# Where six of the first sixteen weight sums run: out of the recurrence and the first MLP, into the output projection

## The chip, the cores and the metric

One core of one Trainium2 chip runs the whole program. The metric is the device time of one execution in microseconds; lower is better. The kernel before took 2056.83 us, the median of three runs (2054.85, 2056.83 and 2059.17 us).

## The reference

A trunk of two layers on one sequence of 1024 tokens with 1024 features, all in float32. Layer 0 mixes tokens by a gated linear recurrence (HGRN2), layer 1 by a Conformer convolution module. Each mixer is followed by a squared-ReLU MLP with 4096 hidden features.

```python
def reference(x, ...):
    for i in range(DEPTH):                       # DEPTH = 2
        if i % N_MIXERS == 0:
            mix = hgrn2_mixer(x, a_w_in[j], lb_all[j], a_norm_g[j], a_w_out[j])
        else:
            mix = conformer_conv_mixer(x, ...)
        x = layer_norm(DEEPNORM_ALPHA * x + mix, ln_mix_g[i], ln_mix_b[i])
        ff = jnp.square(jax.nn.relu(x @ ffn_w1[i])) @ ffn_w2[i]
        x = layer_norm(DEEPNORM_ALPHA * x + ff, ln_ffn_g[i], ln_ffn_b[i])
    return x

def hgrn2_mixer(h, w_in, lb, norm_g, w_out):
    ...                                          # chunks of 32, o per head
    o = o * lax.rsqrt(jnp.mean(jnp.square(o), axis=-1, keepdims=True) + RMS_EPS)
    ...
    return o.astype(h.dtype) @ w_out             # "output projection"
```

## The kernel before

Every large product is made in three passes: each operand is split into a high part that TensorE takes in one pass and a low part that holds the rest, and high x high, high x low and low x high are added in PSUM. On top of that the products of the two MLPs and of the recurrence's projections are made by a scheme of the Strassen kind: a product of 2 x 2 blocks becomes seven products ("forms", numbered 1 to 7) of sums of blocks. Forms 1, 2 and 4 take a block of the weight as it is; forms 6, 5, 7 and 3 take sums of two to four blocks.

**Weight sums.** The weights w2 of both MLPs' second products are cut into blocks; there are eight groups (c = 0 to 7) in each layer, four blocks of 128 x 1024 in each group. The four sums of a group are made in DRAM, by DMAs alone. `block_sums` (L402) issues them: two copies of 1 MiB from the weights into the sum's tile (L419, L420), then one addition of 1 MiB onto it (L421) and two additions of 0.5 MiB (L423), which each take what the one before left. [...] Sixteen such sums are made over the program: `to_sum` (L427) lists the eight of layer 0, then the eight of layer 1. Layer 0's are read in the first MLP's second product, from about 850 us on, and layer 1's in the last one, from about 1720 us on.

**Where they are issued.** Twelve in the recurrence: its loop over pairs p and forms i calls `block_sums` at every sixth form (L1022), with a gap of 12 ticks between the parts (a tick is one step of the recurrence's order; `later` puts a job that many ticks ahead). There POOL issues copies and additions alike. Two in the first MLP's loop over c, at c = 0 and c = 2 (L1477), with the copies on SP's queue and the additions on POOL's at once. The last two come later, in the second layer, through the argument `adds`; that is not touched.

**The output projection** (L1206 to L1220) runs over two halves of the tokens, four tiles t of 128 tokens in each and two column halves n: sixteen entries, of which entry 0, 1 and 2 had their product made in the recurrence's last steps (`early_out`). An entry makes a product of 24 matmuls (`w<-oT` in the trace), then DVE evacuates it into y. At n = 1 the layer norm of that tile follows (`x1_block`): statistics on DVE, a power on POOL (`mv<-mv,nhalf`, L518 in the trace, 1.5 us each), two DVE operations `y<-y,mv,ln_mix_g` and `y<-y,mv,ln_mix_b`, a store of y to DRAM for the residual (`kept<-y`, SP's queue), and TensorE transposes of y (`ps<-ident,y`) that become the operand `x1f` of the first MLP. Eight norms, so eight powers.

**Loads ahead.** In the same stretch SP loads the first weights of the first MLP (`raw<-in_w1q_dram`, L90 in `Slots`, L135 in `Forms`), which ACT and DVE split into `fw`; `early[0].ahead(1)` asks for the first of them at entry 9, the others follow at the end of the loop. Then form (0,1), (0,2), (1,1), (1,2) of the first MLP run (the pair is the group c and the form), and its loop goes on with form (0,6), the first one whose weight is a sum (`fw<-sum`), made by DVE from the loads.

**What sets the order.** In the recurrence the order of all engines' queues is the order of the code (`order` opens a manual schedule, closed at L1038). Behind L1038 a scheduler orders each engine's instructions by its own estimates. POOL, as any engine, runs its queue in order: an addition that waits for its copies holds up every power behind it.

Of the kernel before, what the change touches and what calls it, by code (L numbers as in the profile page):

```python
# [8 lines left out]
F32 = mybir.dt.float32  # L9
# [3 lines left out]
ALU = mybir.AluOpType  # L13
PSUM = bass.MemoryType.PSUM

P = 128
# [4 lines left out]
HT = 512  # L21
# [23 lines left out]
ORDER = (1, 2, 6, 5, 7, 3, 4)  # L45
# [66 lines left out]
class Forms(Slots):  # L112
# [12 lines left out]
    def add(self, x, y, out=None):  # L125
        out = self.sums() if out is None else out
        self.vector.tensor_tensor(out=out, in0=x, in1=y, op=ALU.add)
        return out
# [140 lines left out]
def body(ctx, tc, d, out):  # L269
    nc = tc.nc  # L270
    cst = ctx.enter_context(tc.tile_pool(name="cst", bufs=1))
    stat = ctx.enter_context(tc.tile_pool(name="stat", bufs=4))
    dram = ctx.enter_context(tc.tile_pool(name="dram", bufs=1, space=bass.MemoryType.DRAM))
# [6 lines left out]
    def view(kb, shape, dt=F32, name="t"):  # L280
        at, top = int(kb * 1024), KBYTES * 1024
        if at < edge[0]:
            if edge[0] < top:
                space.tile([P, (top - edge[0]) // 4], F32, name="gap")
            edge[0] = 0
        if at > edge[0]:
            space.tile([P, (at - edge[0]) // 4], F32, name="gap")
        edge[0] = at + (prod(shape) + 7) // 8 * 32
        return space.tile([P, *shape], dt, name=name)
# [39 lines left out]
    def acc():  # L329
        return rings["mm"]()  # L330
# [40 lines left out]
    order = ExitStack()  # L371
# [12 lines left out]
    def later(n, job):  # L384
        if n:
            waiting.append((ticks[0] + n, job))
        else:
            job()

    def tick(n=1):  # L390
        for _ in range(n):
            ticks[0] += 1
            for at, job in [w for w in waiting if w[0] <= ticks[0]]:
                waiting.remove((at, job))
                job()

    sums = {}

    def block_sums(name, layer, c, after=None, gap=0, adds=None):

        t = sums[name, layer, c] = dram.tile([4, P, 1024], F32, name=f"sum_{name}{layer}{c}")
        v, w = t.rearrange("a p n -> p a n"), d[name][layer, c].rearrange("a p n -> p a n")  # L402
        queue = nc.sync if after is not None else nc.gpsimd
        if adds is not None:

            def copies(rows, after):
                nc.sync.dma_start(out=t[0:4:2, rows.start, 0:1], in_=after)
                queue.dma_start(out=v[rows, 0:2], in_=w[rows, 0:4:2])
                queue.dma_start(out=v[rows, 2:4], in_=w[rows, 0:2])

            copies(slice(16, P), after)
            adds.append(lambda after: copies(slice(0, 16), after))
            adds.append(lambda after: nc.gpsimd.dma_start(out=v[:, 0:2], in_=w[:, 2:4], accum_op=ALU.add))
            for i in (2, 3):
                adds.append(lambda after, i=i: nc.gpsimd.dma_start(out=v[:, i], in_=v[:, i - 1], accum_op=ALU.add, max_dma_last_dim=4096))
            return
        if after is not None:
            nc.sync.dma_start(out=t[0:4:2, 0, 0:1], in_=after)
        queue.dma_start(out=v[:, 0:2], in_=w[:, 0:4:2])  # L419
        later(gap // 2, lambda: queue.dma_start(out=v[:, 2:4], in_=w[:, 0:2]))  # L420
        parts = [lambda: nc.gpsimd.dma_start(out=v[:, 0:2], in_=w[:, 2:4], accum_op=ALU.add)]  # L421
        for i in (2, 3):
            parts.append(lambda i=i: nc.gpsimd.dma_start(out=v[:, i], in_=v[:, i - 1], accum_op=ALU.add, max_dma_last_dim=4096))  # L423
        for i, part in enumerate(parts):
            later((i + 1) * gap, part)

    to_sum = [(*of, c) for of in (("w2", 0), ("w2", 1)) for c in range(NFC)]  # L427

# [72 lines left out]
    for k in range(4):  # L501
        c = slice((k % 2) * HT, (k % 2 + 1) * HT)
# [380 lines left out]
    def step():  # L883
        if recs and (not active or len(active) == 1 and active[0][2] >= LAG):
            active.append([recs[0], recurrence(recs.pop(0)), 0])
        if not active:
            return False
        if not (len(active) == 1 and active[0][0] == H - 1 and active[0][2] >= LAG):
            alone[0] = not alone[0]
            if alone[0]:  # L890
                return True
        for one in list(active):
            one[2] += 1

            def go(one=one):
                if next(one[1], one) is one:
                    active.remove(one)

            later(1 if one is not active[0] and one[2] <= 6 else 0, go)
        return True  # L900
# [68 lines left out]
    def seam():  # L969
        plan = [  # L970
            (5, lambda: fetch(0, 0)), (15, lambda: split_w(0, 0, 136)), (17, lambda: split_w(0, 1, 144)), (19, lambda: split_w(0, 3, 120)),
            (21, lambda: split_w(0, 2, 152)), (13, lambda: heads_in(0, 0, 4, 32)), (19, lambda: heads_in(0, 4, 6, 32)),
            (24, lambda: split_heads(0, 0)), (26, lambda: split_heads(0, 2)), (29, lambda: split_heads(0, 4)),
            (16, lambda: bring(0)), (17, lambda: bring(1)), (27, lambda: last_in(H - 2, 0, sixth[0])), (36, lambda: last_in(H - 1, 0, lastly[0])),
            (21, lambda: heads_in(1, 0, 6, 64)), (38, lambda: split_heads(1, 0)), (41, lambda: split_heads(1, 2)), (44, lambda: split_heads(1, 4)),
            (25, lambda: fetch(1, 80)), (39, lambda: split_w(1, 0, 112)), (42, lambda: split_w(1, 1, 128)),
            (45, lambda: split_w(1, 2, 96)), (47, lambda: split_w(1, 3, 104)),
            (43, lambda: last_in(H - 2, 1, sixth[1])), (46, lambda: last_in(H - 1, 1, lastly[1])),
        ]
        for n, job in plan:  # L980
            later(n, job)
# [25 lines left out]
    for p, (kind, j) in enumerate(PAIRS):  # L1007
        st = {"banks": dict(turn_of)}
        turn_of = {"z": turn_of["a"], "a": turn_of["b"], "b": turn_of["z"]}
        pace[1] = 0.0 if p == 0 else 0.6 if p < 3 else 0.5  # L1010
        if kind == "g" and p < len(PAIRS) - 1:
            to_load += [(2 * j, 0), (2 * j + 1, 1), (2 * j, 1), (2 * j + 1, 0)]
        if p == len(PAIRS) - 1:
            seam()
        for i in ORDER:
            if kind == "q" and i == 2:
                while any(a[0] <= j - 3 for a in active) or recs and recs[0] <= j - 3:
                    tick()
                    step()
            pair_product(p, i, made.pop(0), st)  # L1020
            later(2, make_form)
            if (7 * p + ORDER.index(i)) % 6 == 1 and len(to_sum) > 4:  # L1022
                block_sums(*to_sum.pop(0), gap=12)
        if kind == "q":
            later(4, lambda j=j: recs.append(j))
    early_out = ((0, 0), (1, 0), (2, 0))
# [9 lines left out]
    tick(100)  # L1036
    assert not waiting and not loaded and not to_load and not gates, (waiting, gates)
    order.close()  # L1038
    oT = [o[0] for o in oT]


# [94 lines left out]
    y = [view(160 + 16 * h, (NTB, D), F32, "y") for h in range(2)][::-1]  # L1136
# [57 lines left out]
    def x1_block(half, t):  # L1194
# [8 lines left out]
        if t < NTB - 1:  # L1203
            bg.chores += [lambda: x1_first(t), lambda: x1_second(t)]

    for half in range(2):  # L1206
        for t, n in early_out + ((0, 1), (1, 1), (3, 0), (2, 1), (3, 1)) if half == 0 else [(t, n) for t in range(NTB) for n in range(2)]:
            ps = acc()
            if half or (t, n) not in early_out:
                product(ps, wide(oT[half], t, ws[n]))  # L1210
            yv = y[half][:, t, n * HT : (n + 1) * HT]
            vector.scalar_tensor_tensor(out=yv, in0=yv, scalar=ALPHA, in1=ps, op0=ALU.mult, op1=ALU.add)
            if n == 1:
                if half == 1 and t == 0:
                    early[0].ahead(1)
                x1_block(half, t)
                if half == 0 and t:
                    bg.chore()
    for e in early[1:]:
        e.ahead(2)  # L1220


    def store(layer, c, i, q, src):
# [246 lines left out]
    for c in range(NFC):  # L1470
        for i in ORDER[2 if c < 2 else 0 :]:
            (f,) = fw.take(1)
            fw.ahead(3)
            if (c, i) == (0, 7):
                bg.done()
            up.form(c, i, f)
        if c in (0, 2):  # L1477
            block_sums(*to_sum.pop(0), f[:2, 1, :1].bitcast(F32))
        if c == 0:
            up.settle(1)  # L1480
            hold += [view(208, (2, 1024), F32, "spare"), view(216, (1024,), F32, "next")]


    y = [view(32 + 16 * h, (NTB, D), F32, "y") for h in range(2)]
# [371 lines left out]
    y = [view(kb, (NTB, D), F32, "y") for kb in (88, 112)]  # L1856
# [103 lines left out]
```

## Time and profile before

| | us |
|---|---|
| median of three runs | 2056.83 |
| the profiled execution | 2057.16 |
| its span, first to last instruction | 2055.4 |
| granted TensorE clock, mean | 0.999 |
| TensorE (PE) busy | 2023.6 |
| VectorE (DVE) busy | 1488.1 |
| ScalarE (ACT) busy | 1094.5 |
| GpSimd (POOL) busy | 396.3 |

How to read it: the span runs from the first to the last instruction of the profiled execution, and 1.76 us lie around it. A stretch "85 to 430" is counted in microseconds from the start of the span. The recurrence takes about 85 to 437, the output projection about 437 to 509, the first MLP's first product follows. "Idle before" is the time an engine stood still ahead of an instruction, with what ended it behind the arrow. Lines of DVE and PE read L204, a helper that records them, so they are told apart by the names of their tiles. The share of DMA is the mean busy share of the core's 16 DMA engines.

### The profile page before, as it was taken

How to read it: one execution, taken by the hardware profiler on the slowest of the kernel's cores; microseconds unless marked ns; L12 is line 12 of the kernel's file. 1: busy time of each engine (PE TensorE's matmuls, PEld its weight loads, DVE VectorE, ACT ScalarE, POOL GpSimd, SP SyncE). 2: the span in 40 equal slices, each digit the busy share in tenths (PEclk: the TensorE clock that was granted, in tenths of full speed). 3: DMA queues.
4: the chain of work that ended last, by engine and by line, in shares of the span. 5: the costliest groups of instructions: out<-in, count | busy, mean ns of one | idle time of the engine just before them, and what ended most of it. 6: DMA issues, size and time to landing. Idle time of an engine off the chain costs nothing. (4 is left out here: it accounts for less than half of the span.)

```text
span 2055.4 us, 29649 instructions
## 1 busy us (share of the span) xinstructions
PE 2023.6 (98%) x11144; PEld 1669.0 (81%) x11144; DVE 1488.1 (72%) x1978; ACT 1094.5 (53%) x1725; POOL 396.3 (19%) x405
## 2 busy tenths in 40 slices
PE   8999999999999999999999999999999999999998
PEld 7888887888787888888888888888888878888886
DVE  8698888877856675665567897889589666754456
ACT  5456565631655556444443776498615555443343
POOL 0112232111101000000001798089110000100002
PEclk9999999999999999999999999999999999999999
DMA  4778999842679776989998744496759768995542
GB/s 187 221 201 229 265 254 269 248 183 85 192 268 295 281 282 225 394 329 329 338 335 299 298 185 184 180 351 247 276 216 337 231 225 303 391 292 195 195 154 103
DMA packets 183944, 517.55 MB, mean 252 GB/s; under 512 B 17912, under 2 KB 49784, under 8 KB 182776
## 3 DMA queue, kind: packets, MB, share of 16 engines
q1 hardware_dynamic: 168312, 456.93, 61.7%
q0 software_dynamic: 15488, 58.72, 12.2%
q8 instruction: 87, 1.43, 0.3%
q14 instruction: 57, 0.47, 0.1%
HBM read 380.85 MB, written 201.85 MB: 283 GB/s over the span
## 5 line engine op out<-in xcount | busy, mean ns | idle before, releaser
L204 PE MATMUL ps<-dw,dh 128*128 128x512 f32 x2688 | 611.3, 389 | 0.5 <-DVE dh L204 0.5
L204 PEld LDWEIGHTS ps<-dw,dh 128*128 128x128 f32 x2688 | 504.3, 188 | 105.3 <-DVE dh L204 0.9
L204 PE MATMUL ps<-x1f,fw 128*128 128x512 f32 x1344 | 307.5, 390 | 5.2 <-ACT c L1266 2.3
L204 PEld LDWEIGHTS ps<-x1f,fw 128*128 128x128 f32 x1344 | 251.5, 188 | 59.7 <-issue 2.5
L204 PE MATMUL ps<-xf,fs 128*128 128x512 f32 x1008 | 248.6, 397 | 3.6 <-issue 1.7
L204 POOL TENSOR_TENSOR cb<-cb,prod 128x512 f32<-128x512 f32 x168 | 223.2, 1337 | 13.0 <-ACT prod L1591 2.4
L204 PEld LDWEIGHTS ps<-xf,fs 128*128 128x128 f32 x1008 | 184.0, 188 | 42.6 <-issue 1.9
L204 DVE TENSOR_TENSOR dh<-dh 128x1024 fp32r<-128x1024 f32 x112 | 136.5, 1222 | 109.4 <-ACT dh L72 109.3
L204 DVE SCALAR_TENSOR_TENSOR ps<-u,par,ps 128x512 f32<-128x512 f32 x296 | 206.0, 750 | 10.6 <-ACT ps L1603 9.3
L204 PE MATMUL ps<-xa,wa 128*128 128x512 f32 x864 | 203.3, 392 | 0.2
L72 ACT CAST dh<-dh 128x1024 fp32r<-128x1024 f32 x112 | 117.5, 1051 | 143.9 <-DMA dh<-hf 137.7
L72 ACT CAST dw<-dr 128x1024 fp32r<-128x1024 f32 x112 | 117.4, 1054 | 140.9 <-PE ps L204 125.5
L204 DVE TENSOR_TENSOR dw<-dr,dw 128x1024 fp32r<-128x1024 f32 x112 | 136.3, 1223 | 76.6 <-ACT dw L72 75.8
L204 PEld LDWEIGHTS ps<-xa,wa 128*128 128x128 f32 x864 | 160.3, 188 | 33.6 <-DMA wa<-ready 0.6
L1591 ACT ACTIVATE prod<-u,par 128x512 f32<-128x512 f32 x168 | 119.4, 726 | 34.2 <-POOL cb L204 33.5
L518 POOL TENSOR_TENSOR mv<-mv,nhalf 128x1 f32<-128x1 f32 x32 | 42.2, 1321 | 405.1 <-DVE mv L204 394.8
L204 PE MATMUL ps<-w,oT 128*128 128x512 f32 x384 | 89.9, 392 | 1.3 <-ACT oT L932 0.8
L204 PE MATMUL ps<-xb,wa 128*128 128x512 f32 x384 | 91.1, 393 | 0.0
L204 PE MATMUL ps<-vw,xf 128*128 128x512 f32 x336 | 79.9, 400 | 5.6 <-ACT vw L435 5.3
L204 PEld LDWEIGHTS ps<-w,oT 128*128 128x128 f32 x384 | 71.4, 188 | 16.6 <-ACT oT L932 1.2
L204 PEld LDWEIGHTS ps<-xb,wa 128*128 128x128 f32 x384 | 71.1, 188 | 14.3
L204 PEld LDWEIGHTS ps<-vw,xf 128*128 128x128 f32 x336 | 65.0, 194 | 20.1 <-ACT vw L435 5.3
(250 smaller groups left out, 2891.9 us busy)
## 6 DMA issues: line engine op xcount, KB each, us to landing
wa<-ready SPq DMA_DIRECT2D x140, 512.0 KB, 5.0
dh<-hf SPq DMA_DIRECT2D x112, 512.0 KB, 5.3
sum_w<-in_w_dram POOLq DMA_DIRECT2D x40, 1024.0 KB, 10.0
ready<-spare SPq DMA_DIRECT2D x76, 512.0 KB, 5.7
raw<-in_w1q_dram SPq DMA_DIRECT2D x66, 512.0 KB, 4.3
dr<-sum_w SPq DMA_DIRECT2D x64, 512.0 KB, 5.5
hf<-ht SPq DMA_DIRECT2D x112, 256.0 KB, 4.9
dr<-in_w_dram SPq DMA_DIRECT2D x48, 512.0 KB, 5.3
```

Source lines behind the costliest of these rows:

```text
L72: self.nc.scalar.copy(out=slot[:, 0, c], in_=raw[:, c])
L204: return op(*args, **kw)
L518: nc.gpsimd.tensor_tensor(out=dst, in0=src, in1=nhalf[:, :n], op=ALU.pow)
L1591: nc.scalar.activation(tp, u[:, k : k + HT], AF.Copy, scale=tap(j, k))
```

## The change

The recurrence issues eight sums in place of twelve, one at every ninth form, with 18 ticks between the parts. Six sums, layer 1's groups 0 to 5, are issued in the output projection: `sum_parts` cuts a sum into four parts (tiny transfer with both copies, then three additions), and the table `turns` says behind which of the sixteen entries which sum issues its next part. Copies go on SP's queue behind a tiny transfer that reads the y of that entry; additions go on POOL's. POOL alone keeps the code's order there (a second manual schedule, closed behind the loop). The first MLP issues none. The last two sums are as before.

```diff
+    def sum_parts(name, layer, c):
+        t = sums[name, layer, c] = dram.tile([4, P, 1024], F32, name=f"sum_{name}{layer}{c}")
+        v, w = t.rearrange("a p n -> p a n"), d[name][layer, c].rearrange("a p n -> p a n")
+        def copies(after):
+            nc.sync.dma_start(out=t[0:4:2, 0, 0:1], in_=after)
+            nc.sync.dma_start(out=v[:, 0:2], in_=w[:, 0:4:2])
+            nc.sync.dma_start(out=v[:, 2:4], in_=w[:, 0:2])
+        def add(out, x, **kw):
+            return lambda after: nc.gpsimd.dma_start(out=out, in_=x, accum_op=ALU.add, **kw)
+        return [copies, add(v[:, 0:2], w[:, 2:4])] + [add(v[:, i], v[:, i - 1], max_dma_last_dim=4096) for i in (2, 3)]
...
-            if (7 * p + ORDER.index(i)) % 6 == 1 and len(to_sum) > 4:
-                block_sums(*to_sum.pop(0), gap=12)
+            if (7 * p + ORDER.index(i)) % 9 == 1 and len(to_sum) > 8:
+                block_sums(*to_sum.pop(0), gap=18)
...
     order.close()
+    order.enter_context(tc.manual_schedule(engines={mybir.EngineType.Pool}))
...
+    parts, entry = [sum_parts(*to_sum.pop(0)) for _ in range(6)], 0
+    turns = {0: (0,), 2: (1,), 3: (2,), 4: (0,), 6: (0, 1, 3), 7: (2,), 8: (4,), 9: (0, 1, 3, 5), 11: (1, 2, 4), 13: (2, 3, 5), 15: (3, 4, 5)}
     for half in range(2):
...
+            for k in turns.get(entry, ()):
+                parts[k].pop(0)(y[half][:2, t, n * HT : n * HT + 1])
+            entry += 1
+    for k in (4, 5):
+        parts[k].pop(0)(None)
+    assert not any(parts)
     for e in early[1:]:
         e.ahead(2)
+    order.close()
...
-        if c in (0, 2):
-            block_sums(*to_sum.pop(0), f[:2, 1, :1].bitcast(F32))
```

POOL's queue in the output projection, before: the last two norms of the recurrence (`ss`), then the eight powers one behind the other, and the first MLP's work (`x1f` casts and its first sum).

```order
L736 TENSOR_SCALAR ss<-ss 128x4 [waits Activation_49]
L518 TENSOR_TENSOR ss<-ss,nhalf 128x4 [waits Pool_49]
L518 TENSOR_TENSOR mv<-mv,nhalf 128x1 [waits DVE_49] x4
L518 TENSOR_TENSOR mv<-mv,nhalf 128x1 [waits DVE_49,Pool_49] x4
L1191 CAST x1f_4506<-fw 128x1 [waits DMAHW1_49,DMAHW0_49,DMAHW5_49,DVE_49,PE_49]
```

The same place after (L533 is the power now; `sum_w_4491` to `sum_w_4496` are the six sums; DMAHW is a transfer of SP's queue, DMASW one of POOL's), from the first two powers to the sixth:

```order
L533 TENSOR_TENSOR mv<-mv,nhalf 128x1 [waits DVE_49] x2
L438 DMA sum_w_4491<-in_w_dram 128x2x1024 [waits DMAHW1_49,DMAHW0_49]
L533 TENSOR_TENSOR mv<-mv,nhalf 128x1 [waits DVE_49]
L438 DMA sum_w_4491<-sum_w_4491 128x1024 [waits DMAHW2_49,DMASW0_49]
L438 DMA sum_w_4492<-in_w_dram 128x2x1024 [waits DMAHW4_49,DMAHW3_49]
L533 TENSOR_TENSOR mv<-mv,nhalf 128x1 [waits DVE_49]
L438 DMA sum_w_4493<-in_w_dram 128x2x1024 [waits DMAHW7_49,DMAHW1_49]
L533 TENSOR_TENSOR mv<-mv,nhalf 128x1 [waits DVE_49,Pool_49]
L438 DMA sum_w_4491<-sum_w_4491 128x1024 [waits DMASW4_49,DMASW1_49]
L438 DMA sum_w_4492<-sum_w_4492 128x1024 [waits DMAHW5_49,DMASW2_49]
L438 DMA sum_w_4494<-in_w_dram 128x2x1024 [waits DMAHW4_49,DMAHW0_49]
L533 TENSOR_TENSOR mv<-mv,nhalf 128x1 [waits DVE_49,Pool_49]
```

Additions, each of which waits for transfers, now stand ahead of the third power and of every later one. Three more stand ahead of the seventh and three ahead of the eighth; five follow the eighth.

SP's queue after, from the copies of the second sum on (L433 is the tiny transfer, L434 and L435 are the copies; those of the first sum stand just ahead); `kept<-y` are the residual's stores, `raw` at L90 is the first MLP's first weight block:

```order
L434 DMA sum_w_4492<-in_w_dram 128x2x1024 [waits DMAHW4_49,DMAHW3_49]
L435 DMA sum_w_4492<-in_w_dram 128x2x1024 [waits DMAHW5_49]
L1121 DMA kept_4326<-y 128x1024 [waits DMAHW6_49,DVE_49]
L433 DMA sum_w_4493<-y 2x1 [waits DMAHW7_49]
L1121 DMA kept_4326<-y 128x1024 [waits DVE_49]
L434 DMA sum_w_4493<-in_w_dram 128x2x1024 [waits DMAHW7_49,DMAHW1_49]
L435 DMA sum_w_4493<-in_w_dram 128x2x1024 [waits DMAHW2_49]
L1121 DMA kept_4326<-y 128x1024 [waits DVE_49]
L433 DMA sum_w_4494<-y 2x1 [waits DMAHW4_49]
L90 DMA raw<-in_w1q_dram 128x1024 [waits DMAHW5_49,PE_49]
L1121 DMA kept_4326<-y 128x1024 [waits DMAHW6_49,DVE_49]
```

Before, the four stores and the load stood there alone; now three sums' copies and a fourth sum's tiny transfer are ahead of the load, and the copies of the other three sums stand between it and the next loads.

DVE's queue around the split of that load (`fw<-raw,fw`), of before and then of after, from the fourth norm on:

```order
L204 SCALAR_TENSOR_TENSOR y<-y,mv,ln_mix_b 128x1024 [waits DVE_49,Pool_49]
L204 TENSOR_TENSOR fw<-raw,fw 128x1024 [waits DMAHW3_49,Activation_49]
L204 TENSOR_TENSOR x1f_4508<-ps,x1f_4508 128x4x128 [waits Activation_49]
L204 TENSOR_TENSOR x1f_4509<-ps,x1f_4509 128x4x128 [waits Activation_49]
L204 SCALAR_TENSOR_TENSOR y<-y,ps 128x512 [waits PE_49]
```

```order
L204 TENSOR_TENSOR x1f_4487<-ps,x1f_4487 128x4x128 [waits Activation_49]
L204 SCALAR_TENSOR_TENSOR y<-y,ps 128x512 [waits PE_49]
L204 BN_STATS bs<-y 128x6 [waits DVE_49]
L204 TENSOR_TENSOR x1f_4486<-ps,x1f_4486 128x4x128 [waits Activation_49]
L204 TENSOR_TENSOR x1f_4487<-ps,x1f_4487 128x4x128 [waits Activation_49]
L204 TENSOR_TENSOR fw<-raw,fw 128x1024 [waits DMAHW5_49,Activation_49]
L204 SCALAR_TENSOR_TENSOR y<-y,ps 128x512 [waits PE_49]
```

The split moved back by one evacuation and two pairs of `x1f` splits, to just ahead of entry 9's evacuation. On TensorE the transposes of the last tile, which stood some fifty matmuls into form (0,2), now stand ahead of that form's first matmul.

## The prediction

> **What bounds the kernel now.** I read the page first (the span, the busy shares, the DMA queues), then the waits by stretch, then the timelines of the stretch into which the six sums move.
>
> ```profile
> span 2055.4 us, 29649 instructions
> PE 2023.6 (98%) x11144; PEld 1669.0 (81%) x11144; DVE 1488.1 (72%) x1978; ACT 1094.5 (53%) x1725; POOL 396.3 (19%) x405
> q1 hardware_dynamic: 168312, 456.93, 61.7%
> q0 software_dynamic: 15488, 58.72, 12.2%
> sum_w<-in_w_dram POOLq DMA_DIRECT2D x40, 1024.0 KB, 10.0
> ```
>
> TensorE is busy for 98% of the span, and the change neither adds nor removes a matmul. So all that it can win is some of the 31.8 us in which PE is idle, and all that it can lose is new idle time of PE. The two queue rows give the price of a sum. SP's queue (q1) took 61.7% of 2055.4 us, 1268 us of all 16 engines, for 456.93 MB: 2.78 us a MB. POOL's queue (q0) took 12.2%, 251 us, for 58.72 MB: 24 copies and 16 first additions of 1.05 MB (the x40 of the last row) and 32 additions of 0.52 MB. I price its copies like SP's bytes, 24 x 1.05 x 2.78 = 70 us, which leaves 181 us for 33.5 MB that accumulate: 5.4 us a MB. One sum is then 5.8 us of copies and 11.3 us of additions, **17.1 us** of all 16 engines.
>
> ```profile
> 85.00:430.00 345.00, 336.47 (x3592) 278.44 (x3591) 284.15 (x456) 216.89 (x497) 75.39 (x89) 1.00 0.91 254
> 437.00:530.00 93.00, 93.00 (x443) 77.47 (x442) 73.15 (x110) 20.23 (x32) 11.89 (x8) 1.00 0.24 85
> 530.00:575.00 45.00, 41.69 (x180) 33.29 (x179) 35.62 (x38) 28.51 (x39) 8.02 (x9) 1.00 0.84 243
> ```
>
> These are the stretches (columns: PE, PEld, DVE, ACT, POOL, clock, DMA share, GB/s): the recurrence, the output projection with the first forms of the first MLP, and what follows. In the recurrence the DMA engines are nearly full (0.91) and PE loses 8.5 us. In the output projection they are used for 0.24 and PE, busy for 93.00 of 93.00 us, waits for nothing. Whatever is lost there is new.
>
> **The change part by part.**
>
> *Recurrence: four sums fewer, and each spread 18 instead of 12 ticks a part.* That takes 4 x 17 = 68 us from DMA engines that were busy for 0.91 x 345 = 314 us.
>
> ```profile
> PE ps L204 <- issue: 1.7, 1, 1.7
> PE ps L204 <- DVE state L204: 1.4, 2, 0.9
> PE ps L204 <- ACT t L837: 1.2, 2, 0.9
> PE ps L204 <- ACT o L741: 1.1, 2, 0.7
> PE ps L204 <- ACT oT L932: 0.8, 1, 0.8
> POOL sum_w L423 <- DMA sum_w<-in_w_dram: 101.4, 12, 12.1
> POOL sum_w L423 <- DMA sum_w<-sum_w: 30.0, 7, 5.9
> ```
>
> PE's waits between 85 and 430 us add up to 9.1 us in all their rows. POOL also makes the powers of o's norm (behind the wait for o) and stands 131.4 us in front of additions whose input has not landed. Its wait falls with the longer gap. Within reach are the waits for o, oT, t and state, 1.1 + 0.8 + 1.2 + 1.4 = 4.5 us. I take over half of it, **-2.5 us**, between 0 (the sums that stay meet the same instructions) and -9.1 (every wait goes). A small loss would be possible if the shift put a sum on another load. I hold it for covered by these bounds.
>
> *First MLP: two sums fewer.*
>
> ```profile
> 547.94 8.44 PE L204 MATMUL ps<-x1f,fw 128*128 128x512 f32 x36 [1.47 <-ACT c L1266]
> 657.46 5.73 PE L204 MATMUL ps<-x1f,fw 128*128 128x512 f32 x24 [0.85 <-ACT c L1266]
> 664.27 2.12 PE L204 MATMUL ps<-x1f,fw 128*128 128x512 f32 x8 [1.08 <-DVE c L204]
> 655.87 1.05 ACT L1445 CAST spare<-next 128x1024 fp32r<-128x1024 f32 x1 [3.61 <-DMA next<-in_wpw_dram]
> 622.29 1.18 POOL L421 DMA_DIRECT2D sum_w<-in_w_dram  x1 [15.31 <-DMA sum_w<-in_w_dram]
> 643.88 0.83 POOL L423 DMA_DIRECT2D sum_w<-sum_w  x1 [7.96 <-DMA hf<-ht]
> ```
>
> ACT stood 3.61 us for a load that was late while the second sum's additions, begun at 622 and last issued at 644, ran. Two waits of PE follow. They go: 0.85 + 1.08 = **-1.9 us**. The stall at 547.94 lies inside the first sum's transfers, **-1.5 us**, if nothing takes their place. What is late next there is the subject of the next part.
>
> *Output projection: six sums more.* The engines used 0.24 x 93 = 22 us there. Six sums add 6 x 17.1 = 103 us. So 125 us of transfers are to fit into 93 us: 32 us of them stand over at 530 us, where the next stretch already uses 0.84. What they cost goes by what stands behind them in the queues. SP's queue issues the twelve copies ahead of, and between, eight stores of y and the weights of the first MLP. Before, these were:
>
> ```profile
> kept<-y SPq DMA_DIRECT2D x6, 512.0 KB, 2.6
> raw<-in_w1q_dram SPq DMA_DIRECT2D x6, 512.0 KB, 4.5
> 461.69 0.33 SPq L90 DMA_DIRECT2D raw<-in_w1q_dram  x1
> 465.09 1.05 ACT L72 CAST fw<-raw 128x1024 fp32r<-128x1024 f32 x1 [4.58 <-DMA raw<-in_w1q_dram]
> 516.13 0.42 SPq L135 DMA_DIRECT2D raw<-in_w1q_dram  x1
> 534.90 11.56 PE L204 MATMUL ps<-x1f,fw 128*128 128x512 f32 x48 [1.47 <-ACT fw L72]
> ```
>
> (The first two are the DMA views of 440 to 500 and 500 to 530 us: number, size, median time to landing.) The six loads from 502 on took 4.5 us each, the last was issued at 516.13, and form (0,6), the first one that is built from sums of these loads, began at 534.90. What a load takes beside a sum, the first MLP's own sum shows, between 535 and 545:
>
> ```profile
> sum_w<-in_w_dram SPq DMA_DIRECT2D x2, 1024.0 KB
> raw<-in_w1q_dram SPq DMA_DIRECT2D x3, 512.0 KB, 11.4
> sum_w<-in_w_dram POOLq DMA_DIRECT2D x1, 1024.0 KB, 12.1
> ```
>
> There 4.5 us became 11.4. So SP's loads stand in line with the copies and share the engines with POOL's additions. [...]
>
> The sum goes by bytes. From 437 us until the last of the seven loads lands, SP's queue carries twelve copies (12 x 1.05 x 2.78 = 35.0 us), eight stores (8 x 0.524 x 2.78 = 11.7) and seven loads (10.2): 57 us. Of the additions, 6 x 11.3 = 68 us, five of 0.52 MB (5 x 2.83 = 14.2 us) stand behind the last power on POOL; the other 54 us run in between. The last load then lands at 437 + 57 + 54 = 548. A cast (1.05 us in the row of ACT), the sums of loads that DVE makes and a split later, by my estimate some 5 us, form (0,6) begins at 553 instead of 534.9: **+18 us**. If only two thirds of the additions come in between, 45 us, it begins at 544, +9. If all do, at 567, +32, and with the waits of SP and POOL in front of each transfer some us more, +34. Below nothing there is no room: PE waited for nothing there.
>
> This cost has two nearer steps. POOL makes the eight powers of the norms, and additions now stand between them:
>
> ```profile
> 465.17 1.29 DVE L204 SCALAR_TENSOR_TENSOR y<-y,mv,ln_mix_b 128x1024 f32<-128x1024 f32 x1 [0.44 <-POOL mv L518]
> 463.62 1.51 POOL L518 TENSOR_TENSOR mv<-mv,nhalf 128x1 f32<-128x1 f32 x1 [4.82 <-DVE mv L204]
> 476.81 1.45 POOL L518 TENSOR_TENSOR mv<-mv,nhalf 128x1 f32<-128x1 f32 x1 [11.67 <-DVE mv L204]
> 510.83 1.45 POOL L518 TENSOR_TENSOR mv<-mv,nhalf 128x1 f32<-128x1 f32 x1 [10.33 <-DMA raw<-in_w1q_dram]
> 523.21 0.60 PE L204 MATMUL ps<-ident,y 128*128 128x128 f32 x4
> ```
>
> Power four at 463.62 is waited for by DVE within 0.44 us. An addition ahead of a power waits for its copy or for the addition before it (12.1 us above), while the powers lie 6 to 14 us apart. Each late power holds DVE at y<-y,mv, and behind it the evacuation that frees PE's bank. The last row's transposes came at 523.21, well behind the power at 510.83; they now stand ahead of form (0,2), so this slack is nearly gone. And the first load, issued at 461.69, landed by 465.09 with its split directly behind norm four; the split now stands just ahead of an evacuation, behind three sums' copies on SP's queue. If it lands 11.4 us after its issue or later, DVE stops there. I do not add these stalls to the 18 us: PE that is late here finds its loads landed sooner, so both are parts of one delay.
>
> [...]
>
> *Sum:* -2.5 - 1.9 - 1.5 + 18 = +12.1 us on the profiled execution's 2057.16 us, 2069.3. It lies 0.3 us above the median of the runs, so I leave the forecast at **2069.5 us**. 2062 to 2080 goes by +10 to +28 in the output projection.
>
> **The rivals.**
>
> *It fits.* The copies use the 71 free us of 437 to 530, additions run beside them, and loads and powers arrive within their slack. [...] Only the gains stay: -2.5 - 1.9 - 1.5, 2051, and 2048 with more of the recurrence's 9.1 us. Chance 0.22.
>
> *A small loss eats the gains.* The backlog reaches the loads, yet only the last ones, +5: 2056 to 2057, the time before. Chance 0.13.
>
> *The forecast*, 2062 to 2080: 0.45.
>
> *All the work of the sums lies ahead of the loads.* SP's in-order queue waits in front of copies and all additions come in between: +34 - 6 = +28, 2085. It decides from the point at which the first load lands after about 485 us: the evacuation behind its split then comes 10 us late, and with it every load and store that is gated by later evacuations. Three sums' copies ahead of it (17 us) and a third of their additions would bring it from 462 to there. Chance 0.20.
>
> **How the numbers follow.** Slower than before by more than 0.2% (4.1 us, about what a measurement of this kernel can tell from no change) are the forecast and the last rival, 0.65; within it 0.13; faster 0.22. The range leaves out little below 2050 and above 2086, since both ends have a case of their own.
>
> **What would show it.** In the changed profile: the DMA share between 437 and 530 near 0.9 and still over 0.9 to 560; the raw loads of 440 to 545 at 10 us or more to landing, not 4.5; idle time of DVE ahead of its split of the first load or behind POOL's power; form (0,6)'s matmuls near 553 counted from the same start of the output projection; no waits of PE near 657 and 664; PE's waits of 85 to 430 down from 9.1. I am wrong if the additions run at the copies' 2.78 us a MB (then six sums are 70 us, and there are 71), or if PE's waits of 437 to 560 stay below 5 us.

## The result, and the profile after

The changed kernel takes 2081.55 us (median of four, 2079.64 to 2084.47) where the kernel before takes 2055.84 us (four, 2053.36 to 2059.17): a ratio of 1.0116, 95% interval 1.0098 to 1.0134. The forecast was 2069.5 us in a range of 2050 to 2086. So the side and the range held, and the loss, 25.7 us, is about double the one forecast.

The page of the changed kernel, its span, engines and DMA queues:

```profile
span 2079.0 us, 29644 instructions
PE 2028.6 (98%) x11144; PEld 1674.3 (81%) x11144; DVE 1490.4 (72%) x1978; ACT 1097.4 (53%) x1725; POOL 389.0 (19%) x397
```

TensorE's busy time grew by 5.0 us although it runs the same 11144 matmuls, and its idle time by 18.6 us. Both together are the 23.6 us of the span. The same stretches as before (columns: PE, PEld, DVE, ACT, POOL, clock, DMA share, GB/s):

```profile
85.00:430.00 345.00, 337.14 (x3596) 279.39 (x3595) 284.20 (x456) 216.32 (x497) 56.46 (x69) 1.00 0.72 206
437.00:530.00 93.00, 82.49 (x370) 67.71 (x369) 57.05 (x88) 9.46 (x16) 18.05 (x18) 0.94 0.98 268
530.00:575.00 45.00, 31.25 (x130) 25.01 (x129) 34.81 (x39) 22.56 (x30) 13.98 (x14) 0.81 0.88 229
```

The DMA engines, used for 0.24 of the output projection before, are now full (0.98). PE, which lost nothing there, now stands still for 10.5 of 93 us, and for 13.8 of the 45 us that follow (3.3 before). Where the time came from is read off by taking the n-th matmul of the program in both traces (one profile of each kernel) and subtracting the times:

| stretch of the program (time in the trace of before) | after minus before, us | forecast, us |
|---|---|---|
| start to the end of the recurrence (435) | -0.1 | -2.5 |
| output projection and start of the first MLP (435 to 575) | +28.3 | +18 - 1.5 |
| rest of the first MLP's first product (575 to 730) | -2.6 | -1.9 |
| 730 to 1640 | +0.9 | 0 |
| 1640 to 1750 | -3.7 | 0 |
| 1750 to the end | +1.1 | 0 |

PE's waits of the changed kernel between 437 and 570 us, and what POOL and DVE did at the eight powers (timeline, start and duration in us, idle time before with its releaser):

```profile
PE ps L204 <- ACT xl L1199: 15.6, 2, 10.6
PE ps L204 <- DVE y L204: 5.5, 2, 3.3
PE ps L204 <- ACT fw L72: 3.1, 1, 3.1
```

```profile
457.15 1.52 POOL L533 TENSOR_TENSOR mv<-mv,nhalf 128x1 f32<-128x1 f32 x1 [3.28 <-DVE mv L204]
466.58 0.88 POOL L438 DMA_DIRECT2D sum_w<-sum_w  x1 [7.91 <-DMA sum_w<-in_w_dram]
467.20 1.45 POOL L438 DMA_DIRECT2D sum_w<-in_w_dram  x1
467.94 1.31 POOL L533 TENSOR_TENSOR mv<-mv,nhalf 128x1 f32<-128x1 f32 x1
484.65 1.19 POOL L438 DMA_DIRECT2D sum_w<-in_w_dram  x1 [15.40 <-issue]
485.42 1.02 POOL L533 TENSOR_TENSOR mv<-mv,nhalf 128x1 f32<-128x1 f32 x1
...
535.50 1.18 POOL L438 DMA_DIRECT2D sum_w<-in_w_dram  x1 [2.93 <-issue]
536.24 1.03 POOL L533 TENSOR_TENSOR mv<-mv,nhalf 128x1 f32<-128x1 f32 x1
```

```profile
537.30 1.28 DVE L204 SCALAR_TENSOR_TENSOR y<-y,mv,ln_mix_b 128x1024 f32<-128x1024 f32 x1 [7.36 <-POOL mv L533]
```

```profile
526.87 4.15 PE L204 MATMUL ps<-x1f,fw 128*128 128x512 f32 x17
541.60 2.30 PE L204 MATMUL ps<-ident,y 128*128 128x128 f32 x8 [10.58 <-ACT xl L1199]
547.00 73.35 PE L204 MATMUL ps<-x1f,fw 128*128 128x512 f32 x316 [3.10 <-ACT fw L72]
```

This is one chain: every power from the fourth on starts within a microsecond of an addition (L438) that it stood behind. The eighth starts at 536.24 instead of 510.83, 25.4 us late. DVE had made its input by 528.15 (`mv<-mv`, 528.00 and 0.15 us); the additions at 531.73 and 535.50 went out first. DVE waits 7.36 us for it, then splits and copies follow on DVE and ACT, and PE's transposes come at 541.60 after 10.58 us of idle time. Form (0,6), forecast 18 us late, started at 565.34, 30.4 us later than before. The loads of the first MLP are late too, as the DMA view of 437 to 560 us shows:

```profile
q0 software_dynamic: 3198, 12.05, 53.1%
q1 hardware_dynamic: 5448, 20.45, 45.4%
...
sum_w<-in_w_dram SPq DMA_DIRECT2D x12, 1024.0 KB, 13.1
sum_w<-in_w_dram POOLq DMA_DIRECT2D x6, 1024.0 KB, 13.6
sum_w<-sum_w POOLq DMA_DIRECT2D x12, 512.0 KB, 9.3
kept<-y SPq DMA_DIRECT2D x8, 512.0 KB, 14.1
raw<-in_w1q_dram SPq DMA_DIRECT2D x8, 512.0 KB, 12.6
```

Loads take 12.6 us to land, 4.5 before. The price of a byte was right, by the queues' shares: POOL's additions took 53.1% of 123 us for 12.05 MB, 5.4 us a MB, and SP's queue 45.4% for 20.45 MB, 2.73.

### The profile page after: what moved, and what is told of

Its sections match the earlier page's. It is cut to its first block, busy times and chain, and to the rows that moved or that the text cites. A ratio compares the mean times of both kernels' runs of the same rounds, so it can differ in the third digit from the quotient of the medians.

```text
span 2079.0 us, 29644 instructions
## 1 busy us (share of the span) xinstructions
PE 2028.6 (98%) x11144; PEld 1674.3 (81%) x11144; DVE 1490.4 (72%) x1978; ACT 1097.4 (53%) x1725; POOL 389.0 (19%) x397
## 4 chain that ended last, share of the span: by engine, by line
PE 76%; DVE 8%; issue 6%; DMA 5%; ACT 3%; POOL 2%; SPq 0%; DVEq 0%; POOLq 0%; ACTq 0%
PE ps L204 76%; DMA dh<-hf 1%; POOL cb L204 1%; DMA hf<-ht 1%; DMA vr<-in_wv_dram 1%; DMA raw<-in_w1q_dram 1%; DVE t L204 1%; DVE qk L204 1%; DVE xf L204 1%; DVE y L204 1%; DVE ps L204 0%; DVE ht L204 0%; POOL sum_w L438 0%; DVE vr L204 0%; POOL mv L533 0%
## 5 line engine op out<-in xcount | busy, mean ns | idle before, releaser
L533 POOL TENSOR_TENSOR mv<-mv,nhalf 128x1 f32<-128x1 f32 x32 | 40.3, 1262 | 357.7 <-DVE mv L204 357.7
L204 PEld LDWEIGHTS ps<-w,oT 128*128 128x128 f32 x384 | 72.8, 192 | 17.1 <-ACT oT L947 1.2
```

Source lines behind the costliest of these rows:

```text
L204: return op(*args, **kw)
L533: nc.gpsimd.tensor_tensor(out=dst, in0=src, in1=nhalf[:, :n], op=ALU.pow)
```

## Experiments

Two theories say where the 28.3 us come from. **Theory A**: powers stand behind additions on POOL's in-order queue. **Theory B**: the first MLP's loads stand behind the copies on SP's queue and share the DMA engines with the additions. The last columns of the table are the n-th matmul against the trace of before, as above: at the end of the recurrence, and gained or lost from there to 575 us. The kernel before was timed again beside each group of runs (medians of 2055.84 to 2060.59 us), so the ratios are to be compared and not the medians. The last columns come from one profile of each run; between runs that issue the same eight sums in the recurrence, the recurrence column alone differs by up to 6 us.

| run | median us | ratio to before (95%) | recurrence | 435 to 575 |
|---|---|---|---|---|
| the change | 2081.55 | 1.0116 (1.0098 to 1.0134) | -0.1 | +28.3 |
| powers off POOL | 2076.69 | 1.0081 (1.0059 to 1.0104) | +3.7 | +23.4 |
| loads on ACT's queue | 2081.18 | 1.0098 (1.0076 to 1.0121) | +3.3 | +28.9 |
| additions of 16 of 128 rows | 2051.37 | 0.9967 (0.9953 to 0.9981) | -2.5 | 0.0 |
| copies only | 2049.86 | 0.9958 (0.9941 to 0.9975) | -1.1 | +0.1 |
| additions of 64 of 128 rows | 2059.51 | 0.9999 (0.9986 to 1.0011) | -2.5 | +9.4 |
| copies in the recurrence | 2065.98 | 1.0032 (1.0019 to 1.0045) | +1.5 | +11.4 |
| additions in the first MLP | 2061.76 | 1.0012 (0.9998 to 1.0026) | -2.2 | +0.5 |
| 14 sums in the recurrence | 2089.98 | 1.0149 (1.0130 to 1.0168) | +38.4 | 0.0 |
| 16 sums in the recurrence | 2109.10 | 1.0243 (1.0220 to 1.0266) | +60.1 | +0.5 |
| 12 there, 2 in the projection | 2054.67 | 0.9983 (0.9971 to 0.9995) | -0.1 | 0.0 |
| 10 there, 4 in the projection | 2054.50 | 0.9977 (0.9967 to 0.9987) | -3.0 | +5.0 |
| no sums | 2048.16 | 0.9946 (0.9929 to 0.9964) | -3.2 | 0.0 |

**Powers off POOL.** The eight powers are taken from POOL, with all copies and additions in their places. DVE multiplies by 0.5 instead; the power itself is left out.

```diff
     def power_m_half(dst, src, n):
+        if on_dve[0]:
+            vector.tensor_scalar(out=dst, in0=src, scalar1=0.5, scalar2=None, op0=ALU.mult)
+            return
         nc.gpsimd.tensor_tensor(out=dst, in0=src, in1=nhalf[:, :n], op=ALU.pow)
...
     def x1_block(half, t):
+        on_dve[0] = True
         norm(y[half][:, t, :], g, b)
+        on_dve[0] = False
```

> The changed kernel, with the eight powers of the output projection's norms taken off POOL: DVE multiplies by 0.5 in their place, so the norms are scaled wrongly (the power is left out). Copies and additions stay where they are. Theory A (the loss comes because powers stand behind additions on POOL's in-order queue): PE waits for nothing above 2 us between 437 and 560 us, and the time is 2052 to 2060 us. Theory B (the loss comes because the first MLP's loads and the stores stand behind the copies on SP's queue and share the DMA engines with the additions): loads still take 10 us and more, form (0,6) starts 10 to 18 us late, time 2068 to 2080 us. The scheduler may order some work anew, as it costs the norms otherwise; that is good for about 2 us either way.

Theory A alone would have brought the time back. It stayed at 2076.69 us, in theory B's range. The waits moved: PE now waits for the split of the first loads. Below are PE's waits of 437 to 570, then lines of the timelines: DVE's, where the first load's split stands ahead of an evacuation, as the prediction had it, and SP's next loads with ACT's splits of them, which PE's longest wait stood behind.

```profile
PE ps L204 <- ACT fw L72: 15.0, 1, 15.0
PE ps L204 <- DVE y L204: 3.2, 2, 2.3
PE ps L204 <- ACT x1f L1066: 3.1, 1, 3.1
```

```profile
485.42 1.22 DVE L204 TENSOR_TENSOR fw<-raw,fw 128x1024 fp32r<-128x1024 f32 x1 [12.25 <-ACT fw L72]
513.60 0.55 SPq L90 DMA_DIRECT2D raw<-in_w1q_dram  x1
515.36 0.81 SPq L90 DMA_DIRECT2D raw<-in_w1q_dram  x2
532.67 1.04 ACT L72 CAST fw<-raw 128x1024 fp32r<-128x1024 f32 x1 [10.22 <-DMA raw<-in_w1q_dram]
539.01 1.04 ACT L72 CAST fw<-raw 128x1024 fp32r<-128x1024 f32 x1 [4.81 <-DMA raw<-in_w1q_dram]
```

The median load took 7.8 us to land, not the 10 and more that I expected by theory B. But the loads that PE waited for were issued from 513.60 to 516 us, directly behind a sum's copies, and ACT could split them only at 532.67 and 539.01. No power stands behind an addition here, and PE still loses 23.4 us: theory B is enough by itself for most of the loss. The `x1f` row, 3.1 us, is an exception: that work waits for casts on POOL, the first at 557.59 us, which stand behind the last additions, issued up to 557.06. The scheduler ordered some of PE's and DVE's work anew in this run, so 23.4 and 28.3 aren't to be compared to the microsecond.

**Loads on ACT's queue.** The other half: the twelve first loads no longer stand in SP's line, the powers stay behind the additions.

```diff
...
-            self.nc.sync.dma_start(out=a[-1], in_=ap)
+            on_act[1] -= 1
+            (self.nc.scalar if on_act[1] >= 0 else self.nc.sync).dma_start(out=a[-1], in_=ap)
...
+    on_act[:] = 4, 8
```

(The same for the four blocks in `Slots`.)

> The changed kernel with the first twelve loads of the first MLP (four blocks, eight for the first two groups' sums) issued on ACT's queue, so that they no longer stand in line behind the six sums' copies on SP's; copies, additions and powers are where they were. If the place in SP's line makes the loads late: loads 5 to 9 us to landing. If it is the bytes beside them: still 10 us and more. The powers stay behind the additions on POOL either way: if that alone holds PE back (theory A beside B), the time stays at 2070 to 2084 us though the loads are on time; if it does not, it falls to 2055 to 2066 us.

A load's median went from 12.6 to 9.1 us, so by the median some two fifths of the lateness (12.6 less 4.5) came of the line; I put the rest down to the bytes beside it. PE waits for loads for 3.1 us, as in the changed kernel, and for the powers' chain (`xl`, `y`) for 22.9:

```profile
PE ps L209 <- ACT xl L1205: 18.3, 2, 10.8
PE ps L209 <- DVE y L209: 4.6, 1, 4.6
PE ps L209 <- ACT fw L75: 3.1, 1, 3.1
```

```profile
raw<-in_w1q_dram ACTq DMA_DIRECT2D x7, 512.0 KB, 9.1
```

The time stayed, +28.9 us in the stretch. So theory A makes the whole loss also when the loads are less late; they were not on time here, and no run took away both chains and left the bytes. The two chains run side by side, the loads' 23.4 us long and the powers' 28 us, and the longer one hides most of what the other's removal would win.

**What feeds both.** Two runs leave the order of POOL and SP nearly as it is and take away bytes: additions over 16 of 128 rows, and none at all.

```diff
-        return [copies, add(v[:, 0:2], w[:, 2:4])] + [add(v[:, i], v[:, i - 1], ...) for i in (2, 3)]
+        return [copies, add(v[:16, 0:2], w[:16, 2:4])] + [add(v[:16, i], v[:16, i - 1], ...) for i in (2, 3)]
```

> The changed kernel with each addition in its place on POOL, but over 16 of 128 rows (the sums are wrong in the other rows): every wait for copies is kept, the transfers of the additions shrink to an eighth. If powers are late because additions wait for their copies: the powers from the fifth on stay 5 us and more late, 2062 to 2076 us. If they are late because an addition cannot be issued before earlier additions have landed: powers on time within 3 us, 2052 to 2058 us. By theory B (bytes beside the loads) also 2053 to 2060 us.

For none at all, the additions are taken off their list unused:

```diff
             for k in turns.get(entry, ()):
-                parts[k].pop(0)(y[half][:2, t, n * HT : n * HT + 1])
+                part = parts[k].pop(0)
+                if len(parts[k]) == 3:
+                    part(y[half][:2, t, n * HT : n * HT + 1])
...
     for k in (4, 5):
-        parts[k].pop(0)(None)
+        parts[k].pop(0)
```

> The changed kernel with the six sums' copies alone: their additions are left out, so six groups of layer 1 get unfinished sums. The difference to the run with additions in the first MLP is what the additions cost there. Theory A: 2052 to 2056 us, the time before less the first MLP's waits (1.5 + 1.9 us). Theory B: 2055 to 2065 us, as loads stand behind copies.

Both lose nothing in the stretch, and their times lie a little below the ranges that I had written. With the small additions, where every wait of an addition for its copies is kept, the last power starts at 508.68 (510.83 in the kernel before), after waiting for DVE, not for an addition:

```profile
508.68 1.46 POOL L533 TENSOR_TENSOR mv<-mv,nhalf 128x1 f32<-128x1 f32 x1 [8.18 <-DVE mv L204]
```

```profile
437.00:530.00 93.00, 93.00 (x442) 77.10 (x441) 73.34 (x108) 21.36 (x33) 25.50 (x26) 1.00 0.76 237
```

So the additions' place in POOL's order did not make the powers late by itself here, nor did their wait for copies. The twelve copies, 35 us of the engines by the forecast's price, cost nothing where they stand without additions (+0.1 us in the stretch) or beside small ones (0.0). Beside full additions the stretch lost 28.3 us, so the loss needs the additions' bytes; since both theories forecast no loss for small additions, this run does not tell them apart.

**How the loss goes with the bytes.** Additions over 64 rows (`:64` in the place of `:16` above), and full additions with the twelve copies issued in the recurrence instead:

> The changed kernel with each addition over 64 of 128 rows (the sums are wrong in the other rows): copies and own transfers are 57 us, the additions 34, together 91 of 93 us. Theory B by bytes: little stands over, 2050 to 2058 us. If the loss goes with the bytes of the additions in proportion: half of it, 2062 to 2068 us. Theory A, with one addition waiting for the landing of those before: powers 3 to 8 us late, 2056 to 2066 us.

```diff
...
+            if (7 * p + ORDER.index(i)) % 9 == 5 and len(pre) < 6:
+                pre.append(sum_parts(*six[len(pre)], early=True))
...
```

> The changed kernel with the twelve copies of the six sums issued in the recurrence (on POOL's queue, each at a form of its own) and all eighteen additions where they are, ahead of and between the powers; all sums right. Theory A (additions in front of powers on POOL): still an addition is issued only after earlier ones have landed, so the powers stay late and the loss stays, 2068 to 2080 us. Theory B (bytes ahead of and beside the loads): 68 us of additions and 22 us of own transfers are 90 of 93 us, so nothing or little stands over: 2052 to 2060 us. A mixture would lie between, 2060 to 2068.

By the prices of the forecast they put 91 and 90 us of transfers into 93. They lose 9.4 and 11.4 us, not nothing and not half of 28.3: a mixture, as the second expectation allowed. In both PE waits for the loads (`ACT fw`, 9.0 and 9.2 us in three waits; 0.3 us for others), so theory B begins earlier than theory A. That the first run's time lies in theory A's range is chance: its powers from the fifth on wait for DVE and not for an addition. The second run also shows that the additions' bytes are not the whole cause: with all of them in place, taking the copies out of the stretch brought the loss from 28.3 to 11.4 us. The full loss takes both together. A sum of bytes over the whole stretch is too kind to the loads, I think because six of them are issued in its last third.

**Additions later.** Copies in the output projection, the eighteen additions behind the powers, one at every second form of the first MLP:

```diff
...
             up.form(c, i, f)
+            if c and ORDER.index(i) % 2 and any(parts):
+                next(p for p in parts if p).pop(0)(None)
...
```

> The changed kernel with the twelve copies where they are and all eighteen additions moved behind the last power and the first MLP's casts: one behind every second form of the first MLP from its second group on, in the code's order on POOL. Theory A: powers on time, 2053 to 2060 us, of which the first MLP may lose 1 to 4 us, as its own sums did before. Theory B: only the copies are left beside the loads (35 us of 93), loads 5 to 8 us to landing, 2056 to 2066 us.

The output projection is free (+0.5), against theory B. The first MLP pays, and more than the 1 to 4 us that I allowed: 4.6 us up to 730 and 5.6 from there to 1640. PE's waits between 560 and 900 show where; why ACT was late there I did not follow:

```profile
PE ps L204 <- ACT c L1288: 4.9, 2, 3.7
PE ps L204 <- ACT dh L72: 2.0, 1, 2.0
```

**The recurrence.** Its term in the forecast was bounded by one run, and its room for more sums by two. The first leaves out fourteen sums; the second products of both MLPs take plain blocks of the same size in their place.

```diff
...
-                block_sums(*to_sum.pop(0), gap=18)
+                to_sum.pop(0)
...
-    parts, entry = [sum_parts(*to_sum.pop(0)) for _ in range(6)], 0
+    parts, entry = [[] for _ in range(6)], 0
+    del to_sum[:6]
...
```

> The changed kernel without the first fourteen sums: none in the recurrence, none in the output projection (the second products of both MLPs take plain blocks of w2 in the sums' place, of the same size, so their results are wrong). It gives what the sums in the recurrence cost PE at all. If the recurrence's waits are due to them: PE's waits of 85 to 430 fall from 9.1 us to under 3, time 2042 to 2048 us. If not: waits stay at 6 to 9 us, time 2047 to 2052 us, the same as with small additions.

Fourteen sums in the recurrence, from the kernel before, without the first MLP's two; sixteen is the same with `and to_sum` for the last condition:

```diff
-            if (7 * p + ORDER.index(i)) % 6 == 1 and len(to_sum) > 4:
-                block_sums(*to_sum.pop(0), gap=12)
+            if (7 * p + ORDER.index(i)) % 5 == 1 and len(to_sum) > 2:
+                block_sums(*to_sum.pop(0), gap=10)
...
-        if c in (0, 2):
-            block_sums(*to_sum.pop(0), f[:2, 1, :1].bitcast(F32))
```

> The kernel before, with fourteen sums in the recurrence, one at every fifth form with ten ticks between the parts, none in the output projection and none in the first MLP. If the recurrence's sums cost it nothing that counts (its waits hardly fell when four were taken out): the time before less the first MLP's waits of 1.5 to 4 us, so 0.998 to 0.999 of it. If the recurrence is full: 0 to 8 us slower in the recurrence, ratio 1.000 to 1.003.

> As the run with fourteen, with all sixteen sums in the recurrence, so that the last two, which the second layer makes, go there too. If sums in the recurrence are free: 0.997 to 0.999 of the time before. If the last two, which stand in its last forms, reach into the output projection: powers of the norms wait behind their additions, ratio 1.000 to 1.006.

Without any sum PE's listed waits of 85 to 430 us fall only from 9.1 to 5.6 us, and the recurrence ends 3.2 us earlier. With fourteen it ends 38.4 us later, with sixteen 60.1. I expected at most 8. PE's and POOL's waits in the run with fourteen, 85 to 470 us:

```profile
PE ps L204 <- ACT o L741: 28.3, 7, 9.4
```

```profile
POOL sum_w L423 <- DMA sum_w<-in_w_dram: 128.3, 14, 12.1
POOL sum_w L421 <- issue: 64.7, 11, 6.8
POOL sum_w L423 <- DMA sum_w<-sum_w: 45.8, 12, 5.9
```

It is theory A in another place: the powers of o's norm stand behind additions, and o's users behind them (28.3 us in seven waits; 1.1 in two before, from 85 to 430). POOL's queue carries twelve sums there, one every sixth form, at little cost (3.2 us with none); fourteen, one every fifth form, are too many. The two runs change number and spacing together, and thirteen were not tried. Nor did the last two of sixteen reach into the output projection, as I had thought they might: it loses 0.5 us.

**Fewer sums in the output projection.** Two or four there, without any in the first MLP:

```diff
-            if (7 * p + ORDER.index(i)) % 9 == 1 and len(to_sum) > 8:
-                block_sums(*to_sum.pop(0), gap=18)
+            if (7 * p + ORDER.index(i)) % 6 == 1 and len(to_sum) > 4:
+                block_sums(*to_sum.pop(0), gap=12)
...
+    turns = {0: (0,), 2: (1,), 4: (0,), 6: (0, 1), 9: (0, 1), 11: (1,)}
...
```

> Twelve sums in the recurrence as in the kernel before, two in the output projection with copies and additions as in the changed kernel for its first two sums, none in the first MLP. By bytes 22 + 34 = 56 of 93 us, so nothing stands over and the first MLP's waits (4 us) go: ratio 0.997 to 0.999. If additions in front of powers cost by themselves: 2 to 6 us, which the gains eat, ratio 0.999 to 1.002.

```diff
+            if (7 * p + ORDER.index(i)) % 7 == 1 and len(to_sum) > 6:
+                block_sums(*to_sum.pop(0), gap=14)
...
+    turns = {0: (0,), 2: (1,), 3: (2,), 4: (0,), 6: (0, 1, 3), 7: (2,), 9: (0, 1, 3), 11: (1, 2), 13: (2, 3), 15: (3,)}
...
```

> Ten sums in the recurrence, one at every seventh form with 14 ticks, four in the output projection at the places of the changed kernel's first four, none in the first MLP. By bytes 22 + 68 = 90 of 93 us, as with the copies in the recurrence, which cost some 13 us there: loads 5 to 10 us late, ratio 1.001 to 1.005. If the loss begins only above 93 us: ratio 0.996 to 0.999.

Both beat the kernel before, by 0.17% and 0.23%; each interval leaves out 1, but the two intervals overlap. Four cost 5.0 us in the stretch and win 3.0 in the recurrence and the first MLP's 2.6. Their time lies where I expected it if the loss began only above 93 us of transfers, yet 90 us lost 5.0, so it began below; the gains elsewhere paid for it. Two cost nothing there and win the 2.6; the one profile of that run loses 4.7 us between 730 and 1640, which I did not follow.

## Why the prediction was right in side and short in size

- **Recurrence, -2.5 (0 to -9.1).** -0.1 in the profile of the change. Five profiles with the same eight sums there (the change, small and half additions, copies only, additions in the first MLP) give -0.1 to -2.5, and two more +3.3 and +3.7, so one profile can't tell it. With no sums at all 3.2 us are won, so the bound of -9.1 was too far: waits that a trace lists beside a busy queue were mostly not due to it.
- **First MLP's second sum, -1.9.** Right: -2.6 in every run that has no addition there, whatever else was changed. The run that puts eighteen additions there loses 4.6 us instead.
- **The stall at 547.94, -1.5.** Wrong as a step: the run with copies only has 1.4 us of wait there (at 546.45), for a weight's split, though no addition runs. Small additions has 0.2 us. So the wait comes and goes without the sum.
- **Six sums in the output projection, +18 (+9 to +34).** 28.3. The term was mis-sized, and the step that failed is "PE that is late here finds its loads landed sooner, so both are parts of one delay", by which I priced the loads' chain alone. That the two chains don't add was right (powers off POOL 23.4, loads on ACT's queue 28.9, both 28.3). But the longer one decides, and it was the powers', which I had named and not priced. The loads' chain alone cost more than 18 too (23.4, in one profile). The eighth power can be priced, after the fact, from the same bytes: up to it SP's queue carries twelve copies and seven stores (35.0 + 10.2 us) and POOL's thirteen additions 54 us, so 437 + 99 = 536; it started at 536.24. That this agrees to a fraction of a microsecond is luck: the sum leaves out five loads issued by then (7 us) and counts the thirteenth addition in full (5.7 us), which was issued only at 535.50. Before, its transposes had 12 us of slack (510.83 to 523.21); in the new order they had 5.4 (536.24 to 541.60), filled by the splits and copies between, as the prediction said ("nearly gone") and did not add. It also had only part of what holds an addition back. It named the copies and the addition before; of POOL's 63.8 us of waits ahead of additions up to the eighth power, 38.5 ended with nothing shown that they waited for (last section).
- **A cost left out: the clock.** PE's idle time is not all. After PE's idle time from 531 us on, the clock that was granted to it is half (windows of the changed kernel, the same columns as above):

```profile
535.00:540.00 5.00, 0.00 (x0) 0.00 (x0) 2.69 (x3) 0.77 (x2) 1.77 (x2) 0.50 1.07 298
540.00:545.00 5.00, 2.23 (x8) 1.44 (x8) 4.96 (x9) 1.43 (x3) 0.87 (x1) 0.50 1.05 251
545.00:550.00 5.00, 3.00 (x7) 2.40 (x8) 4.97 (x8) 3.52 (x5) 1.69 (x2) 0.50 1.05 281
550.00:555.00 5.00, 5.00 (x23) 4.09 (x23) 3.67 (x5) 1.58 (x3) 0.00 (x0) 0.99 1.07 253
```

The eight transposes at 541.60 took 2.30 us where eight took 1.03 before. PE's busy time grew by 5.0 us in all, about a fifth of the loss. So the wait of 10.58 us cost more than itself here, 1.27 us by these eight transposes alone. PE works without a gap from 547.00 on, and the clock is 0.50 up to 550 and 0.99 in the next five microseconds. In the kernel before, where PE waits for 3.3 us between 437 and 575, it is 1.00 all through that stretch. The traces show this order of events; what sets the clock they do not show.
- **The rivals.** "It fits" (2051) is refuted by the change. At an eighth of the additions' bytes it is what happens (2051.37 us, where the kernel before took 2058.65 beside it, so that the figure itself agrees by chance). The rival on the far side, 2085 with all additions ahead of the loads, came nearer to the result than the forecast; its mechanism (the first load after 485) wasn't the cause, since DVE's part of the first load's split started at 475.92.
- **The price of a sum.** Right: 17.1 us in the prediction, and the queues' shares of the changed kernel, 2.73 and 5.4 us a MB, give 17 us again. Beside the other transfers an addition of 1 MiB took 13.6 us to land.
- **A slip in the last step.** The profiled execution lies 0.3 us above the median of the runs, so 2069.3 had to become about 2069.0 and not 2069.5. It is nothing beside 12 us.
- **Not forecast and not explained.** 3.7 us were won between 1640 and 1750 us, and 0.9 to 4.0 in every other run. I made no run on it. As it comes wherever the sums lie, the one trace of before may simply be long there; that is not shown.

## What to carry to other kernels

A queue with free time is not a free queue (POOL was busy for 18 of the 93 us, and its eighth power came 25.4 us late): ask what stands behind each transfer on the engine that issues it, and how many bytes must land before the last thing behind it may start. Price every chain that the moved work touches, and take the longest, not the first one found; when two run side by side, an experiment that removes one can show little (28.3 us became 23.4 without the powers' chain), and the one that removes their common source (here the bytes of additions and copies together) tells: at an eighth of the additions' bytes the loss was 0.0. Spread background work until each place's share is below its edge: four sums where six cost 28 us, and two about as well, were worth 0.2%.

## What I had not expected of the hardware

- **Additions wait on POOL for something the trace does not show.** Seven of the additions' waits on POOL (45.2 us) end with nothing shown that they waited for. The 1 MiB addition at 484.65 came after 15.40 us, though its copies had landed by 470.4; the addition issued at 467.20 landed 17.1 us later, at 484.3. In the changed kernel each such addition goes out within half a microsecond of an earlier one's landing, and never with more than 1.5 MiB of additions under way at once. I read that as a limit on what POOL's queue holds, which is a guess that no run shows. The runs with smaller additions bear on it: over 64 rows up to four additions were under way at once, 1.5 MiB again, and over 64 or 16 rows no addition waited in this way. So if there is a limit, it is not one on the number of additions up to four. Nor is it one of bytes alone: in the recurrence of the kernel before, copies and additions of POOL's queue together had 2.5 MiB under way. What is counted stays open, as no run was made for it.

```profile
POOL sum_w L438 <- issue: 45.2, 7, 15.4
POOL sum_w L438 <- DMA sum_w<-sum_w: 16.4, 5, 5.8
```

- **The edge is steep.** From twelve to fourteen sums in the recurrence cost 38 us, more than the two sums' own 34 us of engine time, with the DMA share of 85 to 430 us hardly higher (0.91 before, 0.92). Their spacing changed as well.
